# Hybrid diffusion trunk on one core: exponent differences of both GLA directions in two VectorE operations per level, two routing heads per instruction, gates on two expert tiles at once

## The chip, the core and the metric

The kernel runs on one core of one Trainium2 chip. The metric is the device time of one execution in microseconds (us), the median of several runs. Engines: PE (TensorE), DVE (VectorE), ACT (ScalarE), POOL (GpSimd), and SP, which issues most DMAs.

## What is computed

One step of a two-layer trunk on two streams, 128 context tokens ("ctx") and 512 latent tokens ("lat"), width 1024. Each layer has a token mixer of three branches (a bidirectional chunked gated linear attention "GLA", a short convolution, a windowed attention) and a PEER feed-forward, which routes every token to 8 x 16 of 16384 experts. The parts that the change touches, cut from the reference:

```python
# GLA, each direction: decays accumulate as exponents
b = jnp.cumsum(ac, axis=2)
rel = jnp.where(tri, b[:, :, :, None, :] - b[:, :, None, :, :], -jnp.inf)
att = jnp.einsum('bhtsd,bhsd->bhts', qc[:, :, :, None, :] * jnp.exp(rel), kc)
# PEER routing, per head
cand = (s1[..., :, None] + s2[..., None, :]).reshape(...)
top_s, top_pos = lax.top_k(cand, PEER_TOPK)
eidx = jnp.take_along_axis(cidx, top_pos, axis=-1)
# PEER experts
act = gelu(einsum('td,thkd->thk', xb, u_tab[ib])); out = einsum('thk,thkd->td', gb * act, v_tab[ib])
```

## The kernel before

**Order of the work.** The program is written as Python generators that are stepped beside each other (`bg_add`, `tick`, with rates such as `BG` and `RATE`, lines 133 to 163 and 1252 to 1264). A list scheduler then places each instruction in its engine's queue, and each queue runs in order on the chip. So changing one instruction also moves others.

**GLA of the latent stream** (`gla_core`, line 428, called from `mixer_lat`, line 1184). There are four units per layer, one per head. Each takes 512 tokens in four segments of 128. While unit u runs in `gla_core`, the projections of unit u+1 run from `gla_proj` on PE. `gla_core` scans the decays of both directions (BF forward, PB backward, lines 443 and 444), and copies PB shifted by one into EB (line 446). Then come seven levels with m = 64, 32, ..., 1 (line 454). A level builds E, 128 x 2 x 512 exponent differences, from four subtractions of 256 elements: three on DVE (L462, L464, L465) and one on POOL (L463, since `FL[3]` is 1). ACT takes the exponential of all 1024 (L467). DVE multiplies one half by q (L468), POOL the other by k (L469). PE forms four 128 x 128 products (L473), and DVE copies the masked block into att (L474). E has two buffers, so two levels are in work at once. The context stream runs the same code once per layer: ten calls, 70 levels in all.

**Routing** (`routing_pairs`, line 812): ten calls, one per tile of 128 tokens and layer. For each of 8 heads DVE builds 136 candidates (`cand`, L823 and L826) and takes the 16 largest. Then for 2 x 8 (index half, head) DVE makes a one-hot of 256 elements (`oh`, L846), POOL multiplies it by the key numbers (L848), and DVE sums it (L849). `oh` has two buffers. In layer 1 the calls for the latent tiles stand inline, beside `gate_map` and `u_ahead` (lines 1382 to 1394).

**Dense experts of tiles 1 to 3** (`peer_dense`, line 1039): 64 pairs of expert tiles per layer. `up(i)` fills `da` (128 x 2 x 384, two buffers). For the pairs that were computed ahead it loads `sdr` by DMA (L1055) and applies Gelu (L1056); else it computes both tiles by `u_hidden` and applies Gelu (L1060). DVE then multiplies each tile by its gates G (L1063, twice 384 elements). `split` makes daH on ACT (L110) and daL on DVE (L111), and PE multiplies by the expert values (`down`).

Beside all this `peer_gather` fetches expert rows by indirect DMAs issued on POOL (L917), and DVE reduces them (L922, L934). Weights are split by ACT (L172), DVE (L174) and POOL (L176).

Of the kernel before, what the change touches and what calls it, by code (L numbers as in the profile page):

```python
# [9 lines left out]
F32 = mybir.dt.float32  # L10
# [6 lines left out]
OP = mybir.AluOpType  # L17
# [26 lines left out]
def kernel(ctx: ExitStack, tc: tile.TileContext, A: dict, O: list):  # L44
# [383 lines left out]
    def gla_core(s, l, u, gp, t4n, QK, VV, SG, ZB):  # L428
# [11 lines left out]
        BF = gp.tile([128, 4, 128], F32, name="BF", bufs=1)  # L440
        PB = gp.tile([128, 4, 128], F32, name="PB", bufs=1)
        EB = gp.tile([128, 4, 128], F32, name="EB", bufs=1)
# [3 lines left out]
        V.tensor_copy(EB[:, :, 1:128], PB[:, :, 0:127])  # L446
# [365 lines left out]
    def routing_pairs(t, vals, idxs, rp, qp, out):  # L812
# [8 lines left out]
        for h in range(8):  # L821
            cand = qp.tile([128, 136], F32, name="cand", bufs=1)
            V.tensor_add(cand[:, :128].rearrange("p (a b) -> p a b", b=16),  # L823
                         vf[:, h, 0, :8, None].to_broadcast([128, 8, 16]),
                         vf[:, h, 1, None, :].to_broadcast([128, 8, 16]))
            V.tensor_scalar(cand[:, 128:], vf[:, h, 0, 8:], vf[:, h, 1, 0:1], None, op0=OP.add)  # L826
            top16(top[:, h, :], pos[:, h, :], cand)
            if h % 2:
                yield
# [13 lines left out]
        for q in range(2):  # L843
            for h in range(8):
# [5 lines left out]
                if h % 4 == 3:  # L850
                    yield
# [187 lines left out]
    def peer_dense(s, l, hH, hL, dp, e_g, gout, gp):  # L1039
# [9 lines left out]
        def up(i):  # L1049
# [461 lines left out]
```

## Time and profile before

| | before |
|---|---|
| median of 3 runs | 5828.63 us (5822.93 to 5830.19) |
| the profiled execution | 5830.46 us |
| its span, first to last instruction | 5828.7 us |
[...]
| DMA, mean over the span | 239 GB/s, 1395.14 MB |

The profiled execution is the one from which every row below comes. It took 1.8 us more than its span, and 1.8 us more than the median. Shares of busy time are averages over some fifteen stages with different limits, so the stages are read one by one.

### The profile page before, as it was taken

The numbers are of one execution on the slowest core, as the hardware profiler recorded it, in microseconds if no ns is written. First come the engines' busy times: TensorE is split into PE (matmuls) and PEld (weight loads), VectorE is DVE, ScalarE is ACT, GpSimd is POOL, SyncE is SP. The second block draws the span as 40 slices with busy tenths as digits, with TensorE's granted clock in tenths as the row PEclk, the third lists the DMA queues.
The fourth block names the chain that finished last, engine by engine and source line by source line (L and its number), as shares of the span: only waits on it lengthen the run. The fifth ranks groups of instructions, "written<-read, shape, count | busy, mean of one in ns | idle before, by whom it ended". The sixth has DMA issues, their size and how long they took to land. (4 is left out here: it accounts for less than half of the span.)

```text
span 5828.7 us, 79381 instructions
## 1 busy us (share of the span) xinstructions
PE 5182.8 (89%) x28598; PEld 4504.3 (77%) x28598; DVE 4316.1 (74%) x7923; ACT 2048.9 (35%) x3446; POOL 2681.1 (46%) x2207
## 2 busy tenths in 40 slices
PE   7998799888899998899999787999989778899997
PEld 5887678767788898888777676777777778799876
DVE  3328878878554868887777788788778898777677
ACT  2213334221222125653333333333222356433333
POOL 1215544675210216775444455456752566444322
PEclk9999999999899999999999899999989889999999
DMA  7763356887556557889988533578852667888895
GB/s 279 268 237 114 109 191 220 302 290 255 203 208 240 191 205 270 314 326 321 319 305 312 193 112 125 188 259 296 280 181 93 231 235 258 290 273 278 278 315 207
DMA packets 456714, 1395.14 MB, mean 239 GB/s; under 512 B 42880, under 2 KB 184832, under 8 KB 413312
## 3 DMA queue, kind: packets, MB, share of 16 engines
q1 hardware_dynamic: 303248, 833.73, 40.2%
q0 software_dynamic: 153072, 556.34, 27.9%
q8 instruction: 225, 3.69, 0.2%
q14 instruction: 169, 1.38, 0.1%
HBM read 1275.29 MB, written 114.62 MB: 238 GB/s over the span
## 5 line engine op out<-in xcount | busy, mean ns | idle before, releaser
L917 POOL DMA_INDIRECT grow<-in_peer_v_dram,eidx x512 | 661.8, 1293 | 663.4 <-DVE gacc L934 291.6
L917 POOL DMA_INDIRECT grow<-in_peer_u_dram,eidx x512 | 666.4, 1302 | 567.4 <-DVE gjunk L922 198.3
L934 DVE SCALAR_TENSOR_TENSOR gacc<-grow,gw,gacc 128x1024 f32<-128x1024 f32 x508 | 689.0, 1356 | 91.3 <-DMA grow<-in_peer_v_dram,eidx 85.9
L922 DVE SCALAR_TENSOR_TENSOR gjunk<-grow,gh 128x1024 bf16<-128x1024 f32 x512 | 675.0, 1318 | 74.1 <-DMA grow<-in_peer_u_dram,eidx 65.9
L172 ACT ACTIVATE wh<-wraw 128x1024 fp32r<-128x1024 f32 (+1 forms) x388 | 515.3, 1343 | 540.7 <-PE pa L197 214.5
L174 DVE TENSOR_TENSOR wl<-wraw,wh 128x1408 fp32r<-128x1408 f32 (+2 forms) x388 | 565.9, 1461 | 177.1 <-ACT wh L172 175.6
L196 PE MATMUL acc<-wh,daH 128*128 128x512 f32 x1536 | 615.2, 401 | 60.4 <-ACT daH L110 46.3
L176 POOL TENSOR_TENSOR wl<-wraw,wh 128x640 fp32r<-128x640 f32 (+1 forms) x260 | 375.2, 1445 | 618.7 <-ACT wh L172 599.2
L198 PE MATMUL acc<-wh,daL 128*128 128x512 f32 x1536 | 614.4, 400 | 15.8 <-DVE daL L111 15.7
L197 PE MATMUL acc<-wl,daH 128*128 128x512 f32 x1536 | 610.7, 398 | 0.5 <-DVE wl L174 0.5
L196 PE MATMUL pa<-hH,wh 128*128 128x512 f32 x1312 | 544.3, 415 | 45.0 <-DVE th L746 12.3
L198 PE MATMUL pa<-hH,wl 128*128 128x512 f32 x1312 | 536.5, 410 | 11.7 <-DVE wl L174 11.5
L197 PE MATMUL pa<-hL,wh 128*128 128x512 f32 x1312 | 535.6, 408 | 0.7 <-DVE hL L111 0.7
L196 PE MATMUL po<-hH,uH 128*128 128x384 f32 x1376 | 492.3, 358 | 41.9 <-ACT uH L1014 20.0
L198 PE MATMUL po<-hH,uL 128*128 128x384 f32 x1376 | 478.3, 348 | 28.9 <-DVE uL L1016 28.8
L1014 ACT ACTIVATE uH<-uraw 128x1024 fp32r<-128x1024 f32 x256 | 270.6, 1057 | 590.6 <-PE po L197 201.5
L197 PE MATMUL po<-hL,uH 128*128 128x384 f32 x1376 | 476.1, 346 | 0.0
L196 PEld LDWEIGHTS acc<-wh,daH 128*128 128x128 f32 x1536 | 295.8, 193 | 131.5 <-ACT daH L110 58.4
L1016 DVE TENSOR_TENSOR uL<-uraw,uH 128x1024 fp32r<-128x1024 f32 (+1 forms) x256 | 290.9, 1136 | 115.2 <-ACT uH L1014 108.8
L198 PEld LDWEIGHTS acc<-wh,daL 128*128 128x128 f32 x1536 | 295.5, 192 | 94.1 <-DVE daL L111 32.2
L197 PEld LDWEIGHTS acc<-wl,daH 128*128 128x128 f32 x1536 | 296.4, 193 | 62.0 <-DVE wl L174 1.0
L1063 DVE TENSOR_TENSOR da<-da,G 128x384 f32<-128x384 f32 x256 | 184.1, 747 | 214.3 <-ACT da L1056 208.9
(367 smaller groups left out, 12228.2 us busy)
## 6 DMA issues: line engine op xcount, KB each, us to landing
wraw<-in_w_in_dram SPq DMA_DIRECT2D x168, 1024.0 KB
uraw<-in_u_T_dram SPq DMA_DIRECT2D x256, 512.0 KB
wraw<-in_v_n_dram SPq DMA_DIRECT2D x256, 512.0 KB
wraw<-in_w_mod_dram SPq DMA_DIRECT2D x48, 1024.0 KB
wraw<-in_w_branch_dram SPq DMA_DIRECT2D x48, 1024.0 KB
gdr<-stage SPq DMA_DIRECT2D x24, 2048.0 KB
G<-gdr SPq DMA_DIRECT2D x64, 768.0 KB
sdr<-ust SPq DMA_DIRECT2D x172, 192.0 KB
```

The costliest lines, as they stand in the source:

```text
L172: act(H, raw, AF.Copy)
L174: V.tensor_sub(L[:, :m], raw[:, :m], H[:, :m].bitcast(F32))
L176: nc.gpsimd.tensor_sub(L[:, m:], raw[:, m:], H[:, m:].bitcast(F32))
L196: nc.tensor.matmul(out, aH, bH, start=start, stop=False)
L197: nc.tensor.matmul(out, aH, bL, start=False, stop=False)
L198: nc.tensor.matmul(out, aL, bH, start=False, stop=stop)
L917: nc.gpsimd.indirect_dma_start(out=g, out_offset=None, in_=A[tab + str(l)], in_offset=bass.IndirectOffsetOnAxis(ap=eidx[:, j:j + 1], axis=0))
L922: pin(V.scalar_tensor_tensor(junk, g, 1.0, h, op0=OP.mult, op1=OP.mult, accum_out=w[:, j:j + 1]))
L934: pin(V.scalar_tensor_tensor(acc, g, w[:, j:j + 1], acc, op0=OP.mult, op1=OP.add))
L1014: act(uH, raw, AF.Copy)
L1016: V.tensor_sub(uL[:, :m, :], raw[:, :m, :], uH[:, :m, :].bitcast(F32))
L1063: V.tensor_mul(af, af, G[0][:, :, 2 * (i % 2) + f, :])
```

## The change

`gla_core`: BF, EB and PB become three slices of one tile, B3. With the levels' edges taken from slices 0 and 2 (BF and PB) and the values from slices 0 and 1 (BF and EB), one subtraction of 512 elements serves the upper half of both directions and one the lower half. Both are on DVE. The multiplication by q and k becomes one DVE operation of 1024 elements. POOL has no part in a level any more. The shifted copy moves from DVE to ACT.

`routing_pairs`: two heads per instruction, with the multiplication of the one-hot on DVE. `cand` and `oh` share one buffer.

`peer_dense`: one gate multiplication of 768 elements in place of two of 384.

```diff
-        BF = gp.tile([128, 4, 128], F32, name="BF", bufs=1)
...
+        B3 = gp.tile([128, 3, 4, 128], F32, name="B3", bufs=1)
+        BF, EB, PB = (B3[:, i] for i in range(3))
...
-        V.tensor_copy(EB[:, :, 1:128], PB[:, :, 0:127])
+        act(EB[:, :, 1:128], PB[:, :, 0:127], AF.Copy)
...
-            rf = Bv[:, :, 0, m - 1:m].to_broadcast([128, nb, m])
-            rb = Cv[:, :, 1, 0:1].to_broadcast([128, nb, m])
-            V.tensor_sub(Ev[:, 0, :, 1, :], Bv[:, :, 1, :], rf)
-            (nc.gpsimd if FL[3] else V).tensor_sub(Ev[:, 0, :, 0, :], rb, Cv[:, :, 0, :])
-            V.tensor_sub(Ev[:, 1, :, 0, :], rf, Bv[:, :, 0, :])
-            V.tensor_sub(Ev[:, 1, :, 1, :], Cv[:, :, 1, :], rb)
+            Bv = B3.rearrange("p c s (b h m) -> p c (s b) h m", h=2, m=m)
+            edge = Bv[:, :, :, 0, m - 1]
+            far = lambda x: x[:, :, :, None].to_broadcast([128, 2, nb, m])
+            V.tensor_sub(Ev[:, :, :, 1, :], Bv[:, 0:2, :, 1, :], far(edge[:, 0::2]))
+            V.tensor_sub(Ev[:, :, :, 0, :], far(edge[:, 2::-2]), Bv[:, 1::-1, :, 0, :])
...
-            V.tensor_mul(E[:, 0, :], E[:, 0, :], flat(QK[:, 0]))
-            nc.gpsimd.tensor_mul(E[:, 1, :], E[:, 1, :], flat(QK[:, 1]))
+            V.tensor_mul(Ef, Ef, QK.rearrange("p i s t -> p (i s t)"))
...
-            for h in range(8):
-                oh = qp.tile([128, 16, 16], F32, name="oh", bufs=2)
-                V.tensor_tensor(oh, abf[:, q, h, :, None].to_broadcast([128, 16, 16]),
-                                iota16[:, None, :].to_broadcast([128, 16, 16]), op=OP.is_equal)
-                nc.gpsimd.tensor_mul(oh, oh, xf[:, h, q, None, :].to_broadcast([128, 16, 16]))
-                V.reduce_sum(sel[:, q, h, :], oh, axis=mybir.AxisListType.X)
+            for h in range(0, 8, 2):
+                hs = slice(h, h + 2)
+                oh = qp.tile([128, 2, 16, 16], F32, tag="oh", name="oh", bufs=1)
+                V.tensor_tensor(oh, abf[:, q, hs, :, None].to_broadcast([128, 2, 16, 16]),
+                                iota16[:, None, None, :].to_broadcast([128, 2, 16, 16]), op=OP.is_equal)
+                V.tensor_mul(oh, oh, xf[:, hs, q, None, :].to_broadcast([128, 2, 16, 16]))
+                V.reduce_sum(sel[:, q, hs, :], oh, axis=mybir.AxisListType.X)
...
-            for f in range(2):
-                af = a[:, f, :].rearrange("p (c t) -> p c t", t=32)
-                V.tensor_mul(af, af, G[0][:, :, 2 * (i % 2) + f, :])
+            af = a.rearrange("p f (c t) -> p f c t", t=32)
+            b = 2 * (i % 2)
+            V.tensor_mul(af, af, G[0][:, :, b:b + 2, :].rearrange("p c f t -> p f c t"))
```

Candidates are built for two heads likewise (two additions per two heads in place of four).

The scheduler moves other instructions too. DVE's queue at the start of unit 0's levels in layer 1, before (L443 and L444 are the scans; L477 builds KX, the keys for the state; L922 is a gather row):

```order
L444 SCALAR_TENSOR_TENSOR PB<-reset,LA 128x512
L462 TENSOR_TENSOR E<-BF 128x4x64
L446 COPY EB<-PB 128x4x127
L462 TENSOR_TENSOR E<-BF 128x8x32
L464 TENSOR_TENSOR E<-BF 128x4x64
L464 TENSOR_TENSOR E<-BF 128x8x32
L465 TENSOR_TENSOR E<-EB 128x4x64
L465 TENSOR_TENSOR E<-EB 128x8x32
L477 TENSOR_TENSOR KX<-BF 128x512
L922 SCALAR_TENSOR_TENSOR gjunk,gw<-grow,gh 128x1024
L468 TENSOR_TENSOR E<-E,QK 128x512 x2
```

The same place in the changed program, unit 0 of layer 1 (B is the joint tile; L473 is now KX, L920 the gather row):

```order
L444 SCALAR_TENSOR_TENSOR B_26347<-reset,LA 128x512
L473 TENSOR_TENSOR KX<-B_26347 128x512
L920 SCALAR_TENSOR_TENSOR gjunk,gw<-grow,gh 128x1024
L461 TENSOR_TENSOR E<-B_26347 128x8x64
L461 TENSOR_TENSOR E<-B_26347 128x16x32
L462 TENSOR_TENSOR E<-B_26347 128x8x64
L462 TENSOR_TENSOR E<-B_26347 128x16x32
L496 TENSOR_TENSOR QX<-B_26347 128x512
L174 TENSOR_TENSOR wl<-wraw,wh 128x1408
L465 TENSOR_TENSOR E<-E,QK 128x1024 x2
```

KX and a gather row now stand between the scans and the first subtractions. For two levels the eight DVE operations on E (six subtractions, two multiplications) and the copy became six operations of twice the size.

PE's queue at unit 1's levels in layer 0, before (L473 are a level's four products, here two levels together; L196 to L198 are projections):

```order
L196 MATMUL pa<-wh,hH 128x256
L473 MATMUL pb<-E 128x128 x8
L487 MATMUL pt<-idf,KX 128x128 x8
L197 MATMUL pa<-wl,hH 128x256
L198 MATMUL pa<-wh,hL 128x256
```

and now (L469 are the products):

```order
L196 MATMUL pa<-wh,hH 128x256
L469 MATMUL pb<-E 128x128 x4
L196 MATMUL pa<-wh,hH 128x256
L469 MATMUL pb<-E 128x128 x16
L197 MATMUL pa<-wl,hH 128x256
```

Before, two levels stood together and 40 projection rows followed; now five levels stand with one projection between them.

DVE's queue in the dense stage, before and now, with buffer numbers (each gate multiplication is followed by the daL of the pair before it):

```order
L1063 TENSOR_TENSOR da_24711<-da_24711,G_24645 128x384 x2
L111 TENSOR_TENSOR daL_24652<-da_24644,daH_24651 128x768
L174 TENSOR_TENSOR wl_24665<-wraw_24662,wh_24664 128x896
L922 SCALAR_TENSOR_TENSOR gjunk_17926,gw_17927<-grow_24623,gh_17916 128x1024
L922 SCALAR_TENSOR_TENSOR gjunk_17926,gw_17927<-grow_24669,gh_17916 128x1024
L174 TENSOR_TENSOR wl_24723<-wraw_24720,wh_24722 128x896
L1063 TENSOR_TENSOR da_24776<-da_24776,G_24777 128x384 x2
L111 TENSOR_TENSOR daL_24717<-da_24711,daH_24716 128x768
```

```order
L1061 TENSOR_TENSOR da_24598<-da_24598,G_24599 128x768
L111 TENSOR_TENSOR daL_24536<-da_24531,daH_24535 128x768
L174 TENSOR_TENSOR wl_24549<-wraw_24546,wh_24548 128x896
L932 SCALAR_TENSOR_TENSOR gacc_17523<-grow_24509,gw_17525,gacc_17523 128x1024
L932 SCALAR_TENSOR_TENSOR gacc_17523<-grow_24553,gw_17525,gacc_17523 128x1024
L174 TENSOR_TENSOR wl_24611<-wraw_24608,wh_24610 128x896
L932 SCALAR_TENSOR_TENSOR gacc_17523<-grow_24574,gw_17525,gacc_17523 128x1024
L1061 TENSOR_TENSOR da_24664<-da_24664,G_24599 128x768
L111 TENSOR_TENSOR daL_24605<-da_24598,daH_24604 128x768
```

Nothing moved there: the place of the gates and of daL in the loop is as before.

## Rows read from the trace of the kernel before

**Rows 1.** The page, busy time of each engine over the span
```profile
PE 5182.8 (89%) x28598; PEld 4504.3 (77%) x28598; DVE 4316.1 (74%) x7923; ACT 2048.9 (35%) x3446; POOL 2681.1 (46%) x2207
```

**Rows 2.** Busy time by window, eight stretches from scan L443 to last L474
```profile
477.60:522.30 44.70, 32.04 (x216) 29.15 (x215) 43.09 (x73) 17.09 (x26) 23.93 (x19) 0.92 0.20 71
...
3569.80:3618.50 48.70, 31.42 (x149) 25.13 (x150) 48.39 (x70) 20.57 (x27) 30.58 (x25) 0.86 0.30 97
sum 363.50, PE 256.73 PEld 232.98 DVE 337.68 ACT 143.35 POOL 223.67; mean PE 32.09 PEld 29.12 DVE 42.21 ACT 17.92 POOL 27.96
```

**Rows 3.** The same windows, instructions on tile E alone
```profile
sum 363.50, PE 78.78 PEld 70.26 DVE 175.83 ACT 57.62 POOL 133.19; mean PE 9.85 PEld 8.78 DVE 21.98 ACT 7.20 POOL 16.65
```

**Rows 4.** Groups by line, 437 to 760 us, then 3180 to 3680 us
```profile
L473 PE MATMUL pb<-E 128*128 128x128 f32 x224 | 41.0, 344 | 39.5 <-DVE E L468 33.4 <-POOL E L469 6.0
...
L473 PE MATMUL pb<-E 128*128 128x128 f32 x224 | 37.7, 329 | 44.2 <-DVE E L468 35.7 <-POOL E L469 8.4
```

**Rows 5.** DVE's timeline in unit 1, layer 1: start us, duration us, instruction
```profile
3436.02 0.42 DVE L446 COPY EB<-PB 128x508 f32<-128x508 f32 x1
...
3453.46 0.68 DVE L503 TENSOR_TENSOR QX<-QX,QK 128x512 f32<-128x512 f32 x1
3454.07 1.77 DVE L468 TENSOR_TENSOR E<-E,QK 128x512 f32<-128x512 f32 x1
3455.76 2.70 DVE L174 TENSOR_TENSOR wl<-wraw,wh 128x1408 fp32r<-128x1408 f32 x1
3458.39 0.68 DVE L468 TENSOR_TENSOR E<-E,QK 128x512 f32<-128x512 f32 x1
...
3468.18 0.41 DVE L462 TENSOR_TENSOR E<-BF 128x256 f32<-128x256 f32 x1
```

**Rows 6.** ACT's timeline at the same place
```profile
3435.09 1.28 ACT L505 ACT_TABLE_LOAD   x1
...
3436.50 0.61 ACT L479 ACTIVATE KX<-EB 128x512 f32<-128x512 f32 x1
```

**Rows 7.** Timelines of DVE and POOL in routing, layer 1
```profile
4508.67 1.22 DVE L1016 TENSOR_TENSOR uL<-uraw,uH 128x1024 fp32r<-128x1024 f32 x1
4509.81 0.30 DVE L787 MAX8 top<-cand 128x8 f32<-128x136 f32 x1
...
4514.38 0.75 DVE L846 TENSOR_TENSOR oh<-abf,iota 128x256 f32<-128x256 f32 x2
4515.76 0.42 DVE L849 TENSOR_REDUCE sel<-oh 128x16 f32<-128x256 f32 x1 [0.42 <-POOL oh L848]
4516.44 0.42 DVE L849 TENSOR_REDUCE sel<-oh 128x16 f32<-128x256 f32 x1 [0.27 <-POOL oh L848]
4516.78 0.75 DVE L846 TENSOR_TENSOR oh<-abf,iota 128x256 f32<-128x256 f32 x2
...
4514.94 1.47 POOL L848 TENSOR_TENSOR oh<-oh,xf 128x256 f32<-128x256 f32 x2 [0.93 <-DVE oh L846]
```

**Rows 8.** That stage, 4480 to 4830 us: busy by window, then one group
```profile
4480.00:4830.00 350.00, 278.04 (x1549) 265.39 (x1549) 313.84 (x770) 156.08 (x304) 195.48 (x171) 0.88 0.63 222
L849 DVE TENSOR_REDUCE sel<-oh 128x16 f32<-128x256 f32 x64 | 26.6, 417 | 15.7 <-POOL oh L848 15.3
```

**Rows 9.** The chain of waits in the dense stage, one turn of the loop
```profile
5609.56 4.56 DMA da<-sdr
...
5614.21 0.85 ACT da L1056
...
5615.09 0.04 DVE da L1063
...
5616.03 0.96 DVE daL L111
...
5617.01 5.34 DMA da<-sdr
```

**Rows 10.** The gates' line, 2750 to 3200 us: durations min/median/max in ns
```profile
L1063 DVE TENSOR_TENSOR da<-da,G x94: 542/552/842, 2752.6 to 3197.1; 128x384 f32<-128x384 f32 x94
```

More of the change, by code (lines that the diff above doesn't have):

```diff
@@ L439, in gla_core @@
         yield
-        BF = gp.tile([128, 4, 128], F32, name="BF", bufs=1)
-        PB = gp.tile([128, 4, 128], F32, name="PB", bufs=1)
-        EB = gp.tile([128, 4, 128], F32, name="EB", bufs=1)
+        B3 = gp.tile([128, 3, 4, 128], F32, name="B3", bufs=1)
+        BF, EB, PB = (B3[:, i] for i in range(3))
         V.tensor_tensor_scan(flat(BF), reset, flat(LA[:, 0]), 0.0, OP.mult, OP.add)
@@ L457, in gla_core @@
             Ev = E.rearrange("p i (b h m) -> p i b h m", h=2, m=m)
-            Bv = BF.rearrange("p s (b h m) -> p (s b) h m", h=2, m=m)
-            Cv = EB.rearrange("p s (b h m) -> p (s b) h m", h=2, m=m)
-            rf = Bv[:, :, 0, m - 1:m].to_broadcast([128, nb, m])
-            rb = Cv[:, :, 1, 0:1].to_broadcast([128, nb, m])
-            V.tensor_sub(Ev[:, 0, :, 1, :], Bv[:, :, 1, :], rf)
-            (nc.gpsimd if FL[3] else V).tensor_sub(Ev[:, 0, :, 0, :], rb, Cv[:, :, 0, :])
-            V.tensor_sub(Ev[:, 1, :, 0, :], rf, Bv[:, :, 0, :])
-            V.tensor_sub(Ev[:, 1, :, 1, :], Cv[:, :, 1, :], rb)
+            Bv = B3.rearrange("p c s (b h m) -> p c (s b) h m", h=2, m=m)
[3 more added lines that the diff above has]
+            V.tensor_sub(Ev[:, :, :, 0, :], far(edge[:, 2::-2]), Bv[:, 1::-1, :, 0, :])
             Ef = E.rearrange("p i t -> p (i t)")
             act(Ef, Ef, AF.Exp, scale=1.0 / TAU)
-            V.tensor_mul(E[:, 0, :], E[:, 0, :], flat(QK[:, 0]))
-            nc.gpsimd.tensor_mul(E[:, 1, :], E[:, 1, :], flat(QK[:, 1]))
+            V.tensor_mul(Ef, Ef, QK.rearrange("p i s t -> p (i s t)"))
             p = pb([128, 4, 128])
@@ L820, in routing_pairs @@
         pos = qp.tile([128, 8, 16], U32, name="pos", bufs=1)
-        for h in range(8):
[L822 to L829, printed above, removed]
+        for h in range(0, 8, 2):
+            hs = slice(h, h + 2)
+            cand = qp.tile([128, 2, 256], F32, tag="oh", name="cand", bufs=1)[:, :, :136]
+            V.tensor_add(cand[:, :, :128].rearrange("p h (a b) -> p h a b", b=16),
+                         vf[:, hs, 0, :8, None].to_broadcast([128, 2, 8, 16]),
+                         vf[:, hs, 1, None, :].to_broadcast([128, 2, 8, 16]))
+            V.tensor_add(cand[:, :, 128:], vf[:, hs, 0, 8:], vf[:, hs, 1, 0:1].to_broadcast([128, 2, 8]))
+            for i in range(2):
+                top16(top[:, h + i, :], pos[:, h + i, :], cand[:, i, :])
+            yield
         pf = qp.tile([128, 8, 16], F32, name="pf", bufs=1)
@@ L843, in routing_pairs @@
         for q in range(2):
-            for h in range(8):
-                oh = qp.tile([128, 16, 16], F32, name="oh", bufs=2)
-                V.tensor_tensor(oh, abf[:, q, h, :, None].to_broadcast([128, 16, 16]),
-                                iota16[:, None, :].to_broadcast([128, 16, 16]), op=OP.is_equal)
-                nc.gpsimd.tensor_mul(oh, oh, xf[:, h, q, None, :].to_broadcast([128, 16, 16]))
-                V.reduce_sum(sel[:, q, h, :], oh, axis=mybir.AxisListType.X)
-                if h % 4 == 3:
+            for h in range(0, 8, 2):
+                hs = slice(h, h + 2)
+                oh = qp.tile([128, 2, 16, 16], F32, tag="oh", name="oh", bufs=1)
[3 more added lines that the diff above has]
+                V.reduce_sum(sel[:, q, hs, :], oh, axis=mybir.AxisListType.X)
+                if h % 4 == 2:
                     yield
```

## The prediction

> **What bounds the kernel now.** The page first. PE is busy for 89% of the span, DVE for 74%, POOL for 46% [rows 1]. Such averages decide nothing, so I read each stage that the change touches: the levels of the GLA, the routing, and the dense experts.
>
> *The levels.* I cut out the eight stretches from a unit's forward scan to its last masked copy (four units, two layers; first, last and sum are shown). They last 363.5 us together. DVE is busy for 337.7 us of them, 93%, PE for 256.7 us, 71%, and POOL for 223.7 us [rows 2]. The reader should see an engine without gaps, and it is not PE. Of DVE's time 175.8 us is work on E, and POOL spends 133.2 us on E beside it [rows 3]. PE for its part idles 39.5 us in layer 0 and 44.2 us in layer 1 in front of a level's products, mostly because DVE is late [rows 4].
>
> Part of DVE's time there is not work. The multiplication of 512 elements took 0.68 us at 3458.39, but 1.77 us at 3454.07, while POOL ran its own half, and the weight split next to it took 2.70 us [rows 5]. The two engines lengthen each other's operations.
>
> *Routing in layer 1.* DVE is busy for 313.8 of 350 us, 90%, PE for 278.0 us, and DVE waits 15.3 us for POOL's multiplication of the one-hots [rows 8].
>
> *The dense stage.* The chain of waits shows a closed loop. A DMA of `da` lands, ACT applies Gelu, DVE multiplies by the gates and then makes daL of the pair before, and only that frees the buffer for the next DMA, at 5617.01 [rows 9]. One turn is about 7.5 us in the rows shown, of which DVE's gates take 0.94 us (5615.09 to 5616.03). The whole kernel makes 86 such turns, one per `sdr` load. In the pairs without a load, the gates are not in such a loop.
>
> **The levels, step by step.** Each of the 56 latent levels loses three subtractions of 256, one multiplication of 512 on DVE, and both POOL operations. It gains two subtractions of 512 and one multiplication of 1024 on DVE.
>
> - A 512-element operation on two SBUF tiles takes 0.68 us. The next one starts 0.61 us after it (3453.46 to 3454.07) [rows 5]. One of 1024 takes 1.22 us, and its successor starts 1.14 us later (4508.67 to 4509.81) [rows 7]. So a level costs DVE 2 x 0.61 + 1.14 = 2.36 us back to back, or 2.58 us counted in full.
> - 56 levels: 132 to 144 us against 175.8 us [rows 3]. I take 138, a saving of 38 us. The eight copies save 8 x 0.42 = 3 us [rows 5]. The other DVE operations in the stretches now meet less of POOL: split and gather rows such as the one of 2.70 us. I count 4 us for that, the same kind of surplus on one or two operations per unit. POOL's remaining work (223.7 - 133.2 = 90.5 us [rows 2, 3]) still lengthens some, and I give those 4 us back. DVE's work falls from 337.7 to about 297 us.
> - What of it reaches the end? If the idle time of the stretches stays at 25.8 us (363.5 - 337.7), they last 323 us: 41 us gained. If DVE's share falls to 88%, as PE's order asks for, it is 337 us: 26 us gained. The order gives a reason for the second. In unit 1 of layer 0, five levels now stand on PE with one projection between them, so PE has nothing to do while DVE makes them. That is one unit of eight, and part of another. I take 36 us. The bounds are 10 (DVE's share falls to 84%) and 50 us (back-to-back durations, and no contention left).
> - The context levels (14 of the 70) run beside projections that keep PE nearly full. I cost them at nothing. Their cover is that work, and without it they would gain some 0.7 us each, 10 us.
>
> **The shifted copy** goes to ACT, 0.61 us for that size [rows 6]. The first level needs it, and ACT's queue still has a table load of 1.28 us ahead [rows 6]. KX and often a gather row stand on DVE in between. A wait of 0 to 1 us remains per unit, eight times. I take +2 us net (between -3 and +6). What is queued behind it on DVE are the subtractions, and behind those ACT and PE.
>
> **Routing.** A pair of heads recurs every 2.40 us (4514.38 to 4516.78): two one-hots on DVE (0.75), two POOL operations (1.47), two sums, with DVE waiting 0.42 and 0.27 us [rows 7]. Afterwards it is three DVE operations of 512 elements, 1.8 to 2.05 us. DVE's own work in a pair rises from about 1.35 to 1.85 us, 4 us per call of eight pairs. The candidates give back 1 to 2 us per call. So DVE gains 2 to 3 us of work in each of ten calls, and loses its waits. In layer 1 that is about +10 us of work against 15.3 us of waits [rows 8]. In layer 0 the latent calls run under PE's work and cost nothing unless PE runs out. I take -5 us, between +9 (all waits turn into others) and -15.
>
> **The gates.** In a turn of the loop 0.94 us becomes one operation of 768 elements. The nearest row is daL, the same size, 0.96 us, less its overlap with the next [rows 9]. That is -0.06 us in 86 turns, -5 us; between 0 and -10. In the pairs without a load the first tile's gates now wait for the second tile's Gelu. The pairs stand ahead of their use on PE, so I cost that at nothing. Without that cover it would be half a microsecond in each of 42 pairs, 20 us.
>
> **Sum.** -36 + 2 - 5 - 5 = -44 us against the profiled 5830.5 us: 5786.5. The median of the runs is 1.8 us lower than that execution. **I predict 5785 us.**
>
> [...] In the last level (m = 1) the subtractions read and write every second word. Before, 256 such elements took 0.41 us (3468.18), while 512 on flat rows took 0.68 us [rows 5]: no more than half of a flat operation and its fixed part. So I count no extra. [...]
>
> **The rivals.**
>
> - *Freed but not passed on* (about 5822 us). The stretches keep their length. A level's chain is subtraction, exponential, multiplication, products, and it has only two buffers; PE's order decides when the products run. Then DVE's idle time grows by the 41 us that it is given, and only +2 - 5 - 5 = -8 us is left. For it: PE's order in layer 0. Against it: 93% busy now [rows 2], and PE waiting for DVE, not the reverse [rows 4].
> [...]
> - *The gate loop gets longer* (slower than before). The joint gates read G in runs of 32 words, with one more dimension. If that went at the rate of the slowest gates seen, 842 ns for 384 [rows 10], one operation would take 1.68 us: +0.74 us in 86 turns, +64 us in place of -5, and 5854 us. It turns the gain into a loss from 0.94 + 39/86 = 1.4 us per operation on. For it: nothing hides in that loop. Against it: the median of the same runs of 32 words is 552 ns [rows 10], the flat rate.
> - *The change is not what runs*: excluded by the changed program's order, where a level has two subtractions and one multiplication on DVE and none on POOL.
>
> **How the numbers follow.** About 0.2% (12 us, 5817 to 5840) is what a measurement of this kernel can tell from no change. My forecast, 0.65, spans 5755 to 5815, from the bounds of its terms (-78 with every term at its lower end, and -13 if the levels give only 10 and the rest stays small). Freed but not passed on: 0.15, and half of it or a little more within 0.2%. Strided: 0.08, still faster. The gate loop or another loss of that size from the moved order: 0.12. Faster 0.74, within 0.2% 0.14, slower 0.12. The range for 8 in 10 runs from 5750 to 5838: it takes the forecast's ends and the first rival, and leaves out the slower one and a little below.
>
> **What would show it.** In the profile after: no POOL operation on E; DVE operations on E at 0.7 us (512) and 1.2 us (1024); the eight stretches at about 325 us together; PE's idle time before the products at about half of 84 us; the sum of the one-hots waiting for nothing; the gates at 0.95 us for 768. I am wrong if the stretches keep 350 us or more, if 1024-element operations take 1.6 us, or if turns of the gate loop are longer.

## The result and the profile after

| | before | changed |
|---|---|---|
| median | 5826.24 us (5822.93 to 5830.19, 4 runs) | 5696.69 us (5689.62 to 5709.70, 4 runs) |
| ratio, 95% interval | | 0.978 (0.976 to 0.980) |
| the profiled execution, its span | 5830.46, 5828.7 us | 5700.02, 5698.2 us |

The kernel is 130 us faster. I had forecast 44 us, with a range that ends at 5750: the sign was right, the size three times too small. The page of the changed kernel, busy times [rows 1]:

```profile
PE 5144.1 (90%) x28598; PEld 4475.9 (79%) x28598; DVE 4257.4 (75%) x7555; ACT 2052.4 (36%) x3456; POOL 2493.1 (44%) x1907
```

POOL lost 188 us, DVE 59 us and PE 39 us of busy time. The same eight stretches of the latents' levels, first, last and sum [rows 2], and the sum of work on E alone [rows 3]:

```profile
469.10:506.40 37.30, 32.45 (x231) 29.95 (x229) 37.16 (x62) 19.72 (x29) 8.52 (x6) 0.95 0.24 85
...
3470.50:3517.20 46.70, 39.99 (x190) 32.76 (x190) 45.86 (x64) 23.14 (x30) 22.93 (x11) 0.89 0.35 115
sum 327.90, PE 260.82 PEld 233.09 DVE 313.17 ACT 151.14 POOL 105.44; mean PE 32.60 PEld 29.14 DVE 39.15 ACT 18.89 POOL 13.18
```

```profile
sum 327.90, PE 70.49 PEld 64.13 DVE 164.85 ACT 57.43; mean PE 8.81 PEld 8.02 DVE 20.61 ACT 7.18
```

I had forecast 325 us; they last 327.9. DVE is busy for 96% of them, and no POOL time on E is left. But DVE's work on E is 164.9 us, where I had taken 138. The groups of the whole run (busy us, mean ns of one, then idle us before them and what ended it); L469 are the products [rows 4], L462 a subtraction, L465 the multiplication, L847 the sum of one-hots, L1061 the gates [rows 10]:

```profile
L469 PE MATMUL pb<-E 128*128 128x128 f32 x560 | 85.7, 305 | 33.6 <-DVE E L465 33.1 <-DVE rstd L216 0.3
L462 DVE TENSOR_TENSOR E<-B 128x512 f32<-128x512 f32 x70 | 58.2, 850 | 0.0
L465 DVE TENSOR_TENSOR E<-E,QK 128x1024 f32<-128x1024 f32 x70 | 91.5, 1328 | 2.9 <-ACT E L464 2.7
L847 DVE TENSOR_REDUCE sel<-oh 128x32 f32<-128x512 f32 x80 | 54.5, 681 | 0.9
L1061 DVE TENSOR_TENSOR da<-da,G 128x768 f32<-128x768 f32 x128 | 148.2, 1158 | 219.6 <-ACT da L1054 210.0 <-ACT da L1058 7.9 <-DMA G<-gdr 1.4
```

So most marks that I had named came out: PE's idle time before the products fell from 86.1 (group below, among the experiments) to 33.6 us in the whole run, and the one-hots' sum waits 0.9 us (41.1 in the same group of before, shown below). Half of the gates took no more than 0.96 us. The operations on E did not come out: 0.85 us on average for 512 elements and 1.33 for 1024, where I had named 0.7 and 1.2. The total was off by 86 us. The marks tested what I had priced, not what I had priced at nothing. A ledger shows that. Its rows are the shifts of the start of the same instruction from one trace to the other, stage by stage:

| stage | forecast, us | measured, us |
|---|---|---|
| GLA of the context, layer 0 | 0 | -9.3 |
| GLA of the latents, layer 0 | -17 | -11.3 |
| rest of the latents' mixer, layer 0 | 0 | -7.3 |
| GLA of the context, layer 1 | 0 | -9.6 |
| merge of the context, with the latents' routing of layer 0 | 0 | -27.4 |
| gate map, layer 0 | 0 | -0.3 |
| dense experts, layer 0 | -2.5 | -12.4 |
| GLA of the latents, layer 1 | -17 | -34.9 |
| routing and gate map, layer 1 | -5 | -20.0 |
| dense experts, layer 1, and the rest | -2.5 | +2.1 |

**The context's levels.** Windows from a context call's first scan to its last masked copy, before (columns: us, PE, PEld, DVE, ACT, POOL busy with counts, granted clock, DMA share, GB/s):

```profile
106.10:172.90 66.80, 55.28 (x386) 46.01 (x385) 35.98 (x58) 17.67 (x29) 22.03 (x24) 0.90 0.58 211
1662.60:1748.50 85.90, 81.49 (x564) 72.52 (x553) 57.78 (x189) 26.10 (x44) 22.64 (x24) 0.96 0.58 205
sum 152.70, PE 136.76 PEld 118.53 DVE 93.76 ACT 43.77 POOL 44.67; mean PE 68.38 PEld 59.27 DVE 46.88 ACT 21.89 POOL 22.34
```

and after:

```profile
105.70:161.70 56.00, 51.89 (x387) 44.36 (x386) 32.63 (x47) 17.84 (x29) 7.58 (x8) 0.97 0.67 249
1633.00:1711.80 78.80, 77.68 (x563) 69.84 (x554) 55.28 (x167) 26.87 (x44) 11.69 (x8) 1.00 0.64 224
sum 134.80, PE 129.57 PEld 114.19 DVE 87.91 ACT 44.71 POOL 19.27; mean PE 64.79 PEld 57.10 DVE 43.95 ACT 22.36 POOL 9.64
```

They are 18 us shorter: 10.7 us of PE's idle time went, and 7.2 us of its busy time, at a higher mean clock. In layer 0 PE was not "nearly full": it was busy for 55.3 of 66.8 us, at a mean granted clock of 0.90. The timeline of before shows one of the causes (start, duration, operation): the weight split stands in DVE's queue behind two multiplications that take 3.71 us, itself takes 2.68, and PE waits for it for 3.32 us.

```profile
114.29 3.71 DVE L468 TENSOR_TENSOR E<-E,QK 128x512 f32<-128x512 f32 x2
117.93 2.68 DVE L174 TENSOR_TENSOR wl<-wraw,wh 128x1408 fp32r<-128x1408 f32 x1
...
120.66 0.79 PE L198 MATMUL pa<-hH,wl 128*128 128x512 f32 x1 [3.32 <-DVE wl L174]
```

After, the split stands ahead of the multiplication, and takes 1.63 us. PE's wait for it is gone. Others went too, such as a wait for ACT's half of the split (3.7 to 1.2 us in layer 0); how those hang on the levels isn't shown.

```profile
112.97 1.63 DVE L174 TENSOR_TENSOR wl<-wraw,wh 128x1408 fp32r<-128x1408 f32 x1 [1.79 <-ACT wh L172]
114.52 4.81 DVE L465 TENSOR_TENSOR E<-E,QK 128x1024 f32<-128x1024 f32 x2
```

**The latents' routing in layer 0.** From the split of the context's last queries in layer 1 to the end of its merge, with 1289 and 1264 matmuls, it took 215 us before and 184 after:

```profile
1900.00:2115.00 215.00, 192.07 (x1289) 184.95 (x1288) 168.54 (x615) 39.30 (x101) 66.19 (x88) 0.94 0.55 199
```

```profile
1863.00:2047.00 184.00, 178.44 (x1264) 172.68 (x1263) 164.75 (x564) 39.26 (x100) 15.58 (x24) 1.00 0.65 232
```

DVE's work is the same within 4 us. What went is PE's idle time (23 to 6 us), and 14 us of its busy time, with 25 matmuls fewer and a mean clock of 1.00 in place of 0.94. Waits in the later part of that stretch before (total us, times, longest):

```profile
PE pa L363 <- DVE th L746: 13.1, 3, 5.2
...
DVE sel L849 <- POOL oh L848: 14.5, 39, 0.6
```

The merge's additions (`th`, L746) stand in the same DVE queue as the one-hots' sum with its 39 short waits, and PE waited for them for up to 5.2 us at a time. After the change neither wait is there.

### The profile page after: what moved, and what is told of

Read it like the earlier page. It is cut to its first block, busy times and chain, and to the rows that moved or that the text cites. A ratio compares the mean times of both kernels' runs of the same rounds, so it can differ in the third digit from the quotient of the medians.

```text
span 5698.2 us, 78492 instructions
## 1 busy us (share of the span) xinstructions
PE 5144.1 (90%) x28598; PEld 4475.9 (79%) x28598; DVE 4257.4 (75%) x7555; ACT 2052.4 (36%) x3456; POOL 2493.1 (44%) x1907
## 5 line engine op out<-in xcount | busy, mean ns | idle before, releaser
L915 POOL DMA_INDIRECT grow<-in_peer_u_dram,eidx x512 | 689.1, 1346 | 675.8 <-DVE gjunk L920 235.8
L932 DVE SCALAR_TENSOR_TENSOR gacc<-grow,gw,gacc 128x1024 f32<-128x1024 f32 x508 | 707.1, 1392 | 94.8 <-DMA grow<-in_peer_v_dram,eidx 89.8
L176 POOL TENSOR_TENSOR wl<-wraw,wh 128x640 fp32r<-128x640 f32 (+1 forms) x260 | 417.0, 1606 | 703.0 <-ACT wh L172 646.9
L920 DVE SCALAR_TENSOR_TENSOR gjunk<-grow,gh 128x1024 bf16<-128x1024 f32 x512 | 678.1, 1324 | 60.8 <-DMA grow<-in_peer_u_dram,eidx 56.6
L196 PE MATMUL acc<-wh,daH 128*128 128x512 f32 x1536 | 610.9, 398 | 60.3 <-ACT daH L110 43.8
L198 PE MATMUL acc<-wh,daL 128*128 128x512 f32 x1536 | 612.7, 399 | 14.6 <-DVE daL L111 14.3
L196 PE MATMUL pa<-hH,wh 128*128 128x512 f32 x1312 | 544.0, 415 | 48.0 <-DVE th L742 12.3
L198 PE MATMUL pa<-hH,wl 128*128 128x512 f32 x1312 | 536.5, 410 | 7.2 <-DVE wl L174 7.2
L196 PE MATMUL po<-hH,uH 128*128 128x384 f32 x1376 | 490.5, 356 | 26.6 <-ACT uH L1012 10.6
L198 PE MATMUL po<-hH,uL 128*128 128x384 f32 x1376 | 476.6, 347 | 18.4 <-DVE uL L1014 18.1
L196 PEld LDWEIGHTS acc<-wh,daH 128*128 128x128 f32 x1536 | 294.2, 192 | 130.6 <-ACT daH L110 55.3
L985 POOL TENSOR_SCALAR ob<-iota,tt,tt 128x128 f32<-128x128 f32 x192 | 299.3, 1564 | 172.6 <-ACT tt L966 91.8
L198 PEld LDWEIGHTS acc<-wh,daL 128*128 128x128 f32 x1536 | 294.2, 192 | 94.3 <-DVE daL L111 33.4
L196 PEld LDWEIGHTS pa<-hH,wh 128*128 128x128 f32 x1312 | 255.3, 195 | 115.6 <-DVE th L742 14.3
## 6 DMA issues: line engine op xcount, KB each, us to landing
gdr<-stage SPq DMA_DIRECT2D x24, 2048.0 KB, 10.4
```

What stands on the lines that cost most here:

```text
L176: nc.gpsimd.tensor_sub(L[:, m:], raw[:, m:], H[:, m:].bitcast(F32))
L196: nc.tensor.matmul(out, aH, bH, start=start, stop=False)
L198: nc.tensor.matmul(out, aL, bH, start=False, stop=stop)
L915: nc.gpsimd.indirect_dma_start(out=g, out_offset=None, in_=A[tab + str(l)], in_offset=bass.IndirectOffsetOnAxis(ap=eidx[:, j:j + 1], axis=0))
L920: pin(V.scalar_tensor_tensor(junk, g, 1.0, h, op0=OP.mult, op1=OP.mult, accum_out=w[:, j:j + 1]))
L932: pin(V.scalar_tensor_tensor(acc, g, w[:, j:j + 1], acc, op0=OP.mult, op1=OP.add))
```

## The experiments

Each kernel's ratio is to runs of the kernel before on the same chip. "Stretches" are the sums from a unit's first scan to its last masked copy, eight of the latents and two of the context.

| kernel | median, us | ratio (95%) | stretches, us |
|---|---|---|---|
| before | 5819.7 to 5831.1 | 1 | 363 + 153 |
| changed | 5696.7 | 0.978 (0.976 to 0.980) | 328 + 135 |
| a_levels | 5747.5 | 0.987 (0.985 to 0.989) | 313 + 136 |
| a_routing | 5771.2 | 0.990 (0.988 to 0.993) | |
| a_gates | 5821.0 | 0.999 (0.998 to 1.001) | |
| a_copy | 5692.5 | 0.978 (0.976 to 0.980) | 311 + 137 |
| b_lev_nopool | 5770.3 | 0.992 (0.990 to 0.994) | 332 + 137 |
| b_lev_pool | 5793.8 | 0.996 (0.995 to 0.998) | 354 + 141 |
| b_rt_nopool | 5794.5 | 0.996 (0.995 to 0.998) | |
| b_rt_pool | 5810.3 | 0.998 (0.997 to 1.000) | |
| c_lev_ctx | 5808.5 | 0.998 (0.997 to 0.999) | 366 + 135 |
| c_rt_l0 | 5791.1 | 0.995 (0.994 to 0.997) | |
| c_rt_3buf | 5840.6 | 1.004 (1.002 to 1.005) | |
| d_lev_pool | 5797.3 | 0.994 (0.992 to 0.995) | 351 + 137 |
| d_lev_pool2 | 5829.3 | 1.001 (1.000 to 1.003) | 376 + 148 |
| d_rt_pool | 5817.2 | 0.997 (0.996 to 0.998) | |
| d_rt_pool2 | 5798.5 | 0.995 (0.993 to 0.997) | |
| i_kx | 5675.1 | 0.975 (0.973 to 0.977) | 297 + 135 |
| i_mg | 5658.4 | 0.971 (0.969 to 0.973) | 297 + 135 |
| i_pl | 5610.7 | 0.964 (0.963 to 0.966) | 289 + 135 |

### Each part alone

The hunks of the change, one at a time: `gla_core` with the copy on ACT (a_levels), `routing_pairs` (a_routing), `peer_dense` (a_gates).

> The kernel before with the levels' part of the change alone: the exponents by two subtractions, one multiplication on DVE, nothing of a level on POOL, the shifted copy on ACT. By the stages of the two traces (change against before: context GLA of both layers -18 us, latent GLA of both layers -45 us) this part should give about -65 us, some 5760 us, if the parts act apart from each other. My forecast on record gave the levels and the copy -34 us: 5792 us. Rival, that the moved order of the whole program did it and not the part: anything from -20 to -110 us, with gains in stages that this part does not touch.

> The kernel before with the routing part alone: two heads per instruction, the one-hots multiplied on DVE. By the stages of the two traces (layer 0: about -27 us between 1900 and 2115 us; layer 1: -19 us) it should give -45 us, some 5780 us. My forecast gave it -5 us: 5821 us. The rival that the gain in layer 0 came from the context GLA that runs just before it, and not from routing: about -20 us, with nothing gained in the layer 0 call.

> The kernel before with the joint gates alone. Forecast on record: -5 us (-0.06 us in 86 turns), 5821 us. The dense stage of the two traces gave -12 us in layer 0 and about 0 in layer 1: by that 5815 us. If the joint gates only delay the first tile, +0 to +20 us.

-78, -54 and -4 us, by the medians. They add up to -136 against the -130 of the whole. The levels and the routing were both priced far too low; the gates alone can't be told from no change, and -5 fits.

The copy back on DVE, in the changed kernel:

```diff
-        act(EB[:, :, 1:128], PB[:, :, 0:127], AF.Copy)
+        V.tensor_copy(EB[:, :, 1:128], PB[:, :, 0:127])
```

> The changed kernel with the shifted copy back on DVE. Forecast on record for the copy's round trip over ACT: +2 us (between -3 and +6), so this kernel would take about 5695 us, 2 us less than the change. If the copy's place on DVE matters more than its wait, since it stands in front of the first level's subtractions (eight copies of 0.42 us, and what they hold up), it is 3 to 5 us slower: about 5701 us. Either is near what a measurement can tell.

4 us less, within what can be told from no change. So no cost or gain of the copy's place can be told. In its trace the same stages start between 16 us earlier and 7 us later than in the changed kernel's: that much the moved order alone does in the middle of the program. Its latents' stretches are 17 us shorter than the changed kernel's, with the same work in the levels, so the length of the stretches alone is no measure of the total.

### Which calls

The levels' part behind `if s.ctx:`, and the routing part for the four latent calls of layer 0 alone.

> The kernel before with the levels' part in the context's GLA alone (14 of the 70 levels), the latents' levels as before. My forecast cost this at nothing, since PE is nearly full there: 5820 us, no difference that a measurement can tell. The theory from the comparison of the two traces (DVE's and POOL's halves of a context level delay the weight split queued behind them, and the projections wait for that split): about -18 us, 8 in layer 0 and 10 in layer 1, 5802 us.

> The kernel before with the routing part in the four latent calls of layer 0 alone, the six other calls as before. My forecast cost this at nothing, since these calls run under PE's work: 5820 us. The theory from the two traces (DVE's wait for POOL's one-hots holds back the bias additions and splits behind it, for which the context layer's PE waits): -27 us, 5793 us, all of it between the start of context layer 1's merge and the start of the gather in layer 0.

-14 us (interval -6 to -17) and -32 us (-20 to -38). Both were "nothing" in my sum. In the first, the context's stretches are as short as with the whole change. In the second, the shift against before grows from -13.7 us at 1970 us to -34.6 at 2070, beside the context's merge, where the theory had put it, and stays there; 8.7 us of it are there at 1900 us already, before the first one-hot of these calls (1916), as 12 us are at 1850 in a_routing: that much isn't the one-hots' doing.

### POOL's share, or the number of instructions?

POOL's two operations of a level put on DVE, nothing merged (b_lev_nopool); then the merged subtractions with the multiplication still divided (b_lev_pool).

```diff
-            (nc.gpsimd if FL[3] else V).tensor_sub(Ev[:, 0, :, 0, :], rb, Cv[:, :, 0, :])
+            V.tensor_sub(Ev[:, 0, :, 0, :], rb, Cv[:, :, 0, :])
...
-            nc.gpsimd.tensor_mul(E[:, 1, :], E[:, 1, :], flat(QK[:, 1]))
+            V.tensor_mul(E[:, 1, :], E[:, 1, :], flat(QK[:, 1]))
```

> The kernel before with the levels' two POOL operations put on DVE as they are: four subtractions of 256 and two multiplications of 512 per level on DVE, nothing merged. Theory 1 (POOL's half is the cost, its hand-off and what the two engines do to each other's durations): most of the 78 us that the levels' part alone gave comes here too, 5755 to 5785 us, though DVE has one subtraction more (0.41 us x 70 = 29 us by flat durations). Theory 2 (fewer and larger instructions are the gain): about as before or slower, 5825 to 5850 us.

> The kernel before with two merged subtractions per level, but the multiplication still in two halves, one of them on POOL. Theory 1 (POOL's half is the cost): gains little, 5805 to 5825 us. Theory 2 (fewer instructions): most of the 78 us, about 5760 us.

-49 and -26 us. Groups of before: products, their weight loads, a multiplication, a subtraction.

```profile
L473 PE MATMUL pb<-E 128*128 128x128 f32 x560 | 94.4, 326 | 86.1 <-DVE E L468 69.1 <-POOL E L469 16.0 <-DVE mT L276 0.7
L473 PEld LDWEIGHTS pb<-E 128*128 128x128 f32 x560 | 83.8, 231 | 98.4 <-POOL E L469 71.3 <-issue 10.5 <-POOL EB L445 8.3
L468 DVE TENSOR_TENSOR E<-E,QK 128x512 f32<-128x512 f32 x70 | 87.5, 1264 | 3.7 <-ACT E L467 3.7
L464 DVE TENSOR_TENSOR E<-BF 128x256 f32<-128x256 f32 x70 | 53.6, 783 | 0.0
```

Without POOL, still six DVE operations a level:

```profile
L473 PE MATMUL pb<-E 128*128 128x128 f32 x560 | 82.8, 301 | 24.3 <-DVE E L469 23.5
L469 DVE TENSOR_TENSOR E<-E,QK 128x512 f32<-128x512 f32 x70 | 57.9, 841 | 0.0
L468 DVE TENSOR_TENSOR E<-E,QK 128x512 f32<-128x512 f32 x70 | 54.6, 790 | 3.9 <-ACT E L467 3.8
L462 DVE TENSOR_TENSOR E<-BF 128x256 f32<-128x256 f32 x70 | 34.6, 496 | 5.7 <-PE pb L473 5.6
```

Merged, with POOL's half:

```profile
L470 PE MATMUL pb<-E 128*128 128x128 f32 x560 | 90.8, 313 | 64.6 <-POOL E L466 36.0 <-DVE E L465 22.7 <-DVE rstd L216 3.9
L465 DVE TENSOR_TENSOR E<-E,QK 128x512 f32<-128x512 f32 x70 | 72.3, 1043 | 7.8 <-ACT E L464 7.8
```

DVE took over 70 x (0.41 + 0.68) = 76 us of work, and its time on E rose by 12 us only, from 220.9 (37.5 + 53.6 + 42.3 + 87.5) to 233.0 us: a multiplication fell from 1264 to 790 ns, since it no longer runs beside POOL's. The other share of the gain is the hand-off. Before, the products' weights waited 71.3 us for POOL's half, and PE idled 86.1 us; here 24.3 us, and with POOL's half still there 64.6 us. In the latents' stretches DVE's busy time fell from 337.7 to 314.9 us and its idle time from 25.8 to 17.0. The merged form gives a smaller gain: -49 and -26 make -75 of the -78. Theory 1 holds for most of it. The -26, in neither theory's range, are not fewer instructions alone, since b_lev_pool also takes POOL's subtraction away.

The same pair for the routing:

> The kernel before with the one-hots' multiplication on DVE, still one head per instruction. Theory 1 (what stands behind DVE's wait for POOL was the cost: the split's subtractions for which PE waits): most of the 54 us that the routing part alone gave, 5775 to 5795 us, though DVE gets 160 multiplications of 256 elements more, some 0.4 us each, 64 us of work. Theory 2 (two heads per instruction is the gain): 5825 to 5860 us.

> The kernel before with two heads per instruction, the multiplication still on POOL. Theory 1: no gain, 5820 us or, since one buffer now holds the one-hots and DVE waits for the whole of POOL's longer operation, slower, up to 5870 us. Theory 2: most of the 54 us, about 5775 us.

-25 and -9 us, the second at the edge of what can be told (its interval reaches 1.000). With two heads per instruction and POOL, the sum waits more than before, 77.5 us in place of 41.1 (before, then b_rt_pool):

```profile
L849 DVE TENSOR_REDUCE sel<-oh 128x16 f32<-128x256 f32 x160 | 66.4, 416 | 41.1 <-POOL oh L848 40.4
L851 DVE TENSOR_REDUCE sel<-oh 128x32 f32<-128x512 f32 x80 | 54.7, 683 | 77.5 <-POOL oh L850 77.5
```

Alone, either half gives less than the -54 us of both. Without POOL, the three DVE operations of the one-hots take 186.1 us in all (64.0 + 61.4 + 60.7); with two heads per instruction as well, 166.7 (56.8 + 55.5 + 54.4).

### The hand-off, or the lengthening?

Three buffers for the one-hots. The tile `ab`, which is read before them, takes a place in the same ring, which the cut leaves out:

```diff
-                oh = qp.tile([128, 16, 16], F32, name="oh", bufs=2)
+                oh = qp.tile([128, 256], F32, tag="oh", name="oh", bufs=3).rearrange("p (a b) -> p a b", b=16)
```

> The kernel before with three buffers for the one-hots instead of two, so that three one-hots stand on DVE ahead of the first sum that waits for POOL; DVE's and POOL's work is that of before. If DVE's wait for the hand-off is the cost: about half of the waits, 20 us of the 41 us that the sums of the one-hots wait in all, go, and with them 10 to 20 us: 5800 to 5810 us. If the lengthening of DVE's operations by POOL's is the cost, or the count of instructions: no difference, 5820 us.

A miss: 18 us slower. The waits stayed, 35.9 us, and the one-hots on DVE went from 431 to 548 ns each. As I read it, three of them in a row now stand beside POOL's multiplications; that wasn't tried apart:

```profile
L846 DVE TENSOR_TENSOR oh<-abf,iota 128x256 f32<-128x256 f32 x160 | 79.5, 548 | 0.0
L849 DVE TENSOR_REDUCE sel<-oh 128x16 f32<-128x256 f32 x160 | 66.4, 416 | 36.2 <-POOL oh L848 35.9
```

Then POOL got its work back, with a result that nobody reads:

```diff
+            nc.gpsimd.tensor_mul(flat(LA[:, 0]), E[:, 1, :], flat(QK[:, 1]))
```

> The levels' part alone, and beside it, after each level's multiplication, one multiplication of 512 elements on POOL, whose result goes into a buffer that is free by then and is read by nobody (work added; the output is unchanged). 70 of these, about 1.6 us each, are POOL's second multiplication of the kernel before in number and size, without anyone behind it. If the hand-off was the cost: as the levels' part alone, 5745 to 5755 us. If the lengthening of DVE's operations by POOL's was the cost: a good half of the 78 us is lost again, 5785 us or more.

> The routing part alone, and beside it four POOL multiplications of 128 elements after each pair's sum, into a scratch buffer that is read by nobody (work added; the output is unchanged): 320 in all, about 0.45 us each, 145 us of POOL, where the kernel before had 130 us of it. If DVE's wait for POOL, and what stands behind it, was the cost: as the routing part alone, 5765 to 5775 us. If the lengthening was the cost: 5790 us or more.

In the first, 44 of the 78 us are lost. But POOL's reading now holds the buffer of E, and DVE's first subtraction waits 10.5 us for it:

```profile
L461 DVE TENSOR_TENSOR E<-B 128x512 f32<-128x512 f32 x70 | 63.2, 912 | 10.6 <-POOL LA L466 10.5
L470 PE MATMUL pb<-E 128*128 128x128 f32 x560 | 83.1, 297 | 50.8 <-DVE E L465 49.7 <-ACT rmod L270 0.8
```

In the second, 40 of 54 us are lost, but POOL's 320 operations took 251 us, not 145. Neither tells the two apart. So once more, reading BF instead of E, and with two operations per pair instead of four:

> As d_lev_pool (the levels' part alone, and one POOL multiplication of 512 elements per level that nobody reads), but the added work reads the scans and the keys instead of E, so that no buffer of a level is held by it. If the lengthening of DVE's operations is the larger cost: 5785 to 5800 us again. If d_lev_pool was slow by its waits for E's buffers (10.5 us) and what stood behind them: 5750 to 5765 us.

> As d_rt_pool, with two POOL multiplications per pair instead of four: 160 of about 0.79 us, 126 us of POOL, where the kernel before had 130 us. If the lengthening is the cost: 5795 to 5810 us. If the hand-off is: 5770 to 5785 us.

Levels, second try:

```profile
L466 POOL TENSOR_TENSOR LA<-B,QK 128x512 f32<-128x512 f32 x70 | 124.1, 1773 | 63.7 <-DVE B L443 51.5 <-DVE rs_u L210 9.4
L484 PE MATMUL pt<-idf,KX 128*128 128x128 f32 x80 | 18.5, 356 | 43.1 <-POOL KX L478 43.0
L470 PE MATMUL pb<-E 128*128 128x128 f32 x560 | 84.4, 301 | 31.5 <-DVE E L465 31.2
L462 DVE TENSOR_TENSOR E<-B 128x512 f32<-128x512 f32 x70 | 66.9, 973 | 0.0
```

All of the gain is gone, in part by another way than either theory had: the added work stands in POOL's queue ahead of the keys' multiplication KX (L478), and PE's transposes wait 43.1 us for that, where they waited 10.4 us with the levels' part alone. DVE's work on E was lengthened by 23 us (208.1 to 230.9), and PE idled 11 us more before the products. In the latents' stretches, 376 us, DVE was busy for 357; with the levels' part alone it was 304 of 313. So there the loss is DVE's time and not its waits. In the routing, 30 of 54 us were lost, within the range of the lengthening. There the two operations with two inputs took 772 and 770 ns in place of 710 and 694, the sum, with one input, no longer than without POOL's work:

```profile
L850 DVE TENSOR_TENSOR oh<-oh,xf 128x512 f32<-128x512 f32 x80 | 61.8, 772 | 0.8
L851 DVE TENSOR_REDUCE sel<-oh 128x32 f32<-128x512 f32 x80 | 54.2, 677 | 0.9
```

For the levels, how the gain divides between hand-off and lengthening stays open: the work given back to POOL delayed POOL's own queue too (PE's waits for KX rose from 10.4 to 43.1 us). That both are there is shown, the lengthening by DVE's durations, the hand-off by PE's waits.

For the routing two stages of the traces tell more. One is the merge in layer 0, from its first to its last `th` or `mg` addition (L746 before; 1407 to 1413 matmuls in each). The other is routing and gate map of layer 1, from its first candidates to the first daH of the dense experts (2406 matmuls in each). Each row is one profiled execution:

| kernel | merge, layer 0, us | PE's waits for DVE's `th` in it, us | routing and gate map, layer 1, us | DVE busy in that, us |
|---|---|---|---|---|
| before | 222.2 | 13.1 | 516.0 | 437.7 |
| changed | 193.0 | none | 496.7 | 435.0 |
| a_routing | 192.3 | none | 496.0 | 434.8 |
| b_rt_nopool | 194.4 | 0.4 | 513.1 | 447.3 |
| b_rt_pool | 217.9 | 13.7 | 503.7 | 428.9 |
| c_rt_3buf | 219.2 | 10.3 | 523.9 | 437.9 |
| d_rt_pool | 200.1 | 5.5 | 521.8 | 454.9 |
| d_rt_pool2 | 196.9 | 3.0 | 509.9 | 447.6 |

In the merge the hand-off is the larger cost. Taking POOL out of it gives 28 of the 30 us with one head per instruction; two heads with POOL's share kept give 4; POOL work that nobody waits for takes back 5 to 8, with POOL busy for 54 and 81 us (61 before). In layer 1, where DVE is the fullest engine, it is the other way round: taking POOL out gives 3 of the 20 us while DVE's work rises by 10, two heads with POOL give 12, and the added POOL work takes back 14 to 26, with DVE busy for 13 to 20 us more than in a_routing.

### Further along the same way

From the changed kernel: the keys' multiplication as one DVE operation (i_kx), the merge's additions on DVE too (i_mg, `FL = (0, 0, 0, 1)`), and the weight splits of the GLA stages wholly on DVE too, but for the context's in layer 1 (i_pl).

```diff
-            nc.gpsimd.tensor_mul(KX[:, i], KX[:, i], QK[:, 1])
+        V.tensor_mul(KX, KX, QK[:, 1, None].to_broadcast([128, 2, 4, 128]))
...
-    PL = (5, 5, 5, 2, 0)
+    PL = (0, 0, 5, 2, 0)
```

> The changed kernel with the last POOL multiplications of the GLA, two of 512 per unit for the state keys, as one of 1024 on DVE. If POOL's hand-off is what costs, as in the levels: each unit's two POOL operations of 1.88 us, one behind the other, become 1.2 us on DVE, and the transposes on PE that wait for them come up to 2.5 us sooner in 10 units: 5675 to 5690 us against 5697. If DVE's own work decides there: +1.2 us in each of 8 units, 5705 us.

> The changed kernel with the state keys' multiplication on DVE (5675 us), and the merge's 64 POOL additions, some of 128 and some of 512 elements, on DVE too. They stand behind DVE's own operation and before ACT's copy for the next projection. If every hand-off to POOL costs as in the levels: 1 us of latency less in those additions that something waits for, some 10 to 20 us, 5655 to 5665 us. If the merge is bound by PE, where the additions were hidden, and DVE has room: no difference, 5675 us; if DVE has none, 64 times some 0.4 us, up to 5700 us.

> The fastest version so far (5658 us), with the weight splits of the GLA stages wholly on DVE: there POOL made 640 of 2048 columns. If POOL's share costs by lengthening DVE's operations more than it takes off DVE, as in the levels (where DVE took over 76 us of flat work for 12 us): 5635 to 5650 us. If the split's longer time on DVE, about 0.8 us in each of some 190, delays PE, which waits for it: 5670 to 5720 us.

Each was faster than the one before it, by 22, 17 and 48 us by the medians (19, 23 and 39 us by the ratios, since the three ran on different chips). i_kx and i_mg came out within a range that was named, i_pl below both of its. The last is 1.5% faster than the change (5610.7 against 5696.7 us). In i_pl a split of 2048 columns takes DVE 2306 ns; in i_mg it took 1840 ns for 1408 of them, beside POOL's 640:

```profile
L174 DVE TENSOR_TENSOR wl<-wraw,wh 128x2048 fp32r<-128x2048 f32 x116 | 267.4, 2306 | 66.0 <-ACT wh L172 65.9
```

```profile
L174 DVE TENSOR_TENSOR wl<-wraw,wh 128x1408 fp32r<-128x1408 f32 x132 | 242.9, 1840 | 93.3 <-ACT wh L172 93.2
```

DVE took over 116 shares of 640 columns, and its busy time of the whole run fell from 4246.1 to 4193.3 us. With so little of POOL's work left beside them, the levels' operations have the flat durations:

```profile
L465 DVE TENSOR_TENSOR E<-E,QK 128x1024 f32<-128x1024 f32 x70 | 83.8, 1219 | 3.1 <-ACT E L464 3.0
L461 DVE TENSOR_TENSOR E<-B 128x512 f32<-128x512 f32 x70 | 47.4, 688 | 2.2 <-PE pb L469 2.0
L462 DVE TENSOR_TENSOR E<-B 128x512 f32<-128x512 f32 x70 | 46.5, 683 | 0.0
```

## Why the prediction was wrong

- **What bounds the stretches**: right. DVE did, and PE waited for it and for POOL. The levels' term, -36, measured 363.5 - 327.9 = -35.6 us in those stretches, but that is luck. Of the 38 us that DVE was to save on E it saved 11 (175.8 to 164.9); its other work there fell by 13.5 us, and its idle time by 11 (25.8 to 14.7), which I had kept or let grow. The levels' part alone took 51 us off these stretches. And the whole stage, ends included, gained 46 us in the ledger.
- **"I cost them at nothing" (the context's levels)**: failed. The cover was "projections that keep PE nearly full". A row that I should have read was the weight split in the same DVE queue: the projections that were to hide the levels get their weights through it, and PE waited 3.3 us for one. I had put the price without cover at 10 us; it was 18 us in the stretches and -14 in c_lev_ctx. Of the 18, 7.2 us are PE's busy time at the higher clock, for which I had no term.
- **"In layer 0 the latent calls run under PE's work and cost nothing unless PE runs out"**: failed, and it is the largest single miss, 27 us. PE did run out: it idled 23 of 215 us there. DVE's waits of 0.3 to 0.6 us are too short to be seen in the list of the longest, but they come 39 times in a queue on which the merge depends. Without them (b_rt_nopool) the merge took 194.4 in place of 222.2 us.
- **Routing in layer 1, -5**: mechanism right, size off. It measured -20 us. I let the added DVE work (+10 us) eat two thirds of the waits (15.3 us). DVE's busy time in routing and gate map did not rise, 442.7 to 440.3 us. Where one head per instruction was kept, in b_rt_nopool, it did rise by 10 us, and the stage gained 3.
- **Lengthening by POOL**: seen, and quoted in two rows [rows 5], then counted for the other operations as 4 us gained and 4 us given back. For all 70 levels DVE's time on E was 220.9 us, where the flat durations give 70 x (3 x 0.41 + 0.68) = 134 us. For the changed levels I took flat durations, as if POOL's remaining work left E alone; it did not (0.85 us for 512 elements, 0.68 to 0.69 in i_pl).
- **The copy, +2; the gates, -5; no extra at m = 1**: right within what can be told. In i_pl the subtractions, m = 1 among them, average 683 and 688 ns, where one level of seven at twice the duration would lift a mean of 683 to 780. So the strided operations of m = 1 were not twice as long, the case to which I gave the chance of 0.08.
- **Open**: 12.4 us in the dense stage of layer 0 and 7.3 us in the mixer of layer 0. The gates alone gave 4 us by the median; what moved the rest wasn't tried apart.
- **The range**: its lower end was built of each priced term's lower end. A term that is put at zero "under cover" needs a lower end too, and I gave it none.

## What to carry to other kernels

Before a term is set to zero because another engine is busy, look up which queue feeds that engine, and whether the instructions in question stand in it: here 39 waits of at most 0.6 us stood in DVE's queue with the merge's additions, and with the one-hots' multiplication on DVE (b_rt_nopool) PE's waits for those additions fell from 13.1 to 0.4 us. And do not count an operation that is divided between DVE and POOL as halved, since DVE's half of 512 elements took 1264 ns beside POOL's and 790 ns without: measure DVE's duration beside POOL and alone, and add the wait of whoever needs both halves. Here DVE took over all of a level and was busy for less. Which of the two counts depends on the stage: beside the merge, where PE was to be kept busy, it was mostly the wait; in layer 1's routing, where DVE was the fullest, DVE's whole time.

## What the runs showed of the hardware

- DVE operations with two SBUF inputs took longer beside POOL's: the 512-element multiplication took 1264 ns on average beside POOL's and 790 ns without (b_lev_nopool), and that of the one-hots 772 ns with POOL's added work (d_rt_pool2) and 710 ns without (a_routing). DVE's sum of one-hots, with one input, was not lengthened (680 ns without POOL's added work, 677 with). POOL's own half of the multiplication took 1259 to 3572 ns in the kernel before, with a median of 1558.
- The mean granted TensorE clock, in shares of full speed, rose from 0.90 to 0.97 and from 0.96 to 1.00 in the context's stretches, where PE's idle time shrank (11.5 to 4.1 and 4.4 to 1.1 us). PE's busy time for the same matmuls (within one of 386 and 564) fell by 3.4 and 3.8 us as well, so more time went than the waits themselves.
- Single steps of two words cost nothing here: in the changed kernel 17 of the 20 subtractions at m = 1, each of 512 elements at every second word, took 669 to 699 ns, where the medians over all seven levels are 680 (L461) and 684 ns (L462). The other three took 1619, 2061 and 2076 ns, each beside POOL's share of a weight split.
